# Sending all of the attention branch's gated output tiles through the seven-product form in a streaming-encoder trunk

## Chip, cores and metric

The kernel runs on one core of a Trainium2 chip. The metric is the device time of one launch in microseconds (us); lower is better.

## What is computed

Two layers over 640 tokens (512 of a new stream and 8 x 16 of running streams) with 1024 features. The part of the reference that matters here is the end of the mixer:

```python
g = jax.nn.sigmoid(g + b_gate)
g_conv, g_attn = jnp.split(g, 2, axis=-1)
y_conv, conv_new = _short_conv(cb, cc, cv, conv_prev, w_conv)
...
m = g_conv * (y_conv @ w_conv_out) + g_attn * (y_attn @ w_attn_out)
return m @ w_o, conv_new, k_new, v_new
```

`y_conv` and `y_attn` have 512 columns; `g_conv`, `g_attn`, `m` and the result have 1024. Ahead of the mixer and behind it stands a SwiGLU block. All is float32.

## The kernel before

**Layout and products.** Features lie on the 128 partitions and tokens on the free axis, so a tile is 128 x 640, split where needed into two token halves of 320. Every operand is split into a rounded part `hi` and a remainder `lo` (ACT casts `hi`, DVE subtracts to get `lo`), and a product is three matmuls (hi·hi, hi·lo, lo·hi). Weights are split on the chip in the same way, slab by slab.

**Seven products.** Most large products are done by Winograd's variant of Strassen's scheme: two output rows by two token halves need seven block products instead of eight. For that the right-hand operand needs, beside its four blocks, four mixtures: `XT5`, `XN6`, `XT7` and `XT4`. The weights need mixtures too: two slabs arrive by DMA, DVE adds halves of them, and a third part is made in DRAM-to-SBUF transfers that accumulate (tile `one`, on POOL's queue).

**The units.** In `outputs` three kinds of units follow each other. A *gate unit* (`gate_pair(m)`, tiles `qa`, `qb`, `qc`) makes two gate tiles by seven block products of 12 matmuls. A *rows unit* (`rows`, tiles `ra`, `rb`, `rc`) makes four output tiles by seven products of 12 matmuls. A plain tile (`out(m)`, tile `py`) takes 24 matmuls. Before, the order from the eighth gate on is: four times a gate unit and two plain tiles of the attention branch. The conv branch has four plain tiles and one rows unit for the other four; that unit stands just ahead of gate unit 8. Behind them `po` (the product with `w_o`) takes the eight mixed tiles `m_0` to `m_7`, 48 matmuls for each output.

**What sets the order.** `outputs` is written in a hand-set order for PE, DVE and ACT: each engine runs its instructions in the order in which the code names them. Within a unit, `prep` casts the next weight slab on ACT, `flush` takes its remainder on DVE, `ahead` adds the halves of a coming slab on DVE, and `at[0..2]` are places in a gate unit (after its first, fourth and fifth product) where the caller hangs other work. `due` runs what an earlier unit put off. SP's queue loads the slabs (`raw`, three buffers and a wait for the oldest to be read), POOL's the `one` tiles (two buffers).

Of the kernel before, what the change touches and what calls it, by code (L numbers as in the profile page):

```python
# [11 lines left out]
F32R = mybir.dt.float32r  # L12
# [4 lines left out]
P = 128  # L17
# [111 lines left out]

# [57 lines left out]
def two(ps):  # L187
    return ps[:, :, :HT]


def halves(t):
    return t.rearrange("p (a b) -> p a b", a=2)
# [3 lines left out]
def trunk(ctx: ExitStack, tc: tile.TileContext, xin, wst, small, pbias, samplebias, kcache, vcache, gfin,  # L196
# [24 lines left out]
    def acc(name):  # L221
        return banks["acc"].tile([P, 2, 512], F32, tag="acc", name=name)
# [1110 lines left out]
    def mixer(l, after):  # L1333
        with tc.tile_pool(name=f"yp{l}", bufs=1, reuse_waits="tile") as yp, \
# [84 lines left out]
            with tc.tile_pool(name=f"gp{l}", bufs=1, reuse_waits="tile") as gp, \  # L1419
                 tc.manual_schedule(engines=ORDERED):  # L1420
# [3 lines left out]
        with tc.manual_schedule(engines=ORDERED):  # L1424
            hold[0] = True
            for m in range(KT):
                po = acc(f"po{l}_{m}")
                product(po, mo)
                ex.weights(m)
                DVE.tensor_tensor(out=halves(x[m]), in0=two(po), in1=halves(x[m]), op=ALU.add)  # L1430
                if m < KT - 1:
                    flush()
                ex.final(m)
        return ex

    class Operands:
# [48 lines left out]
    def outputs(l, gp, X, st, cs, ycp, yas, sigmoid, gates):  # L1485
# [20 lines left out]
        def gate_pair(m, at):  # L1506
            n = f"{l}_{m}"
            pa, pb, pc = (att(f"q{i}{n}")[:, :HT] for i in "abc")
            u, g = gates[m], gates[m + 1] = tmp(f"g{n}"), tmp(f"g{n}_1")
            s0 = quiet()  # L1510
            block(pa, s0, 0, X11, every, True, True)
            ACT.copy(c1, pa)
            due()
            prep(used[0] + 1)
# [9 lines left out]
            ACT.copy(c5, pc)  # L1524
# [4 lines left out]
            DVE.tensor_tensor(out=g[:, t2], in0=g[:, t2], in1=rr[:, t2], op=ALU.mult)  # L1529
# [35 lines left out]
            if post:  # L1565
                post()

        yc, ya, mo = [], [], []
        more = []
        yas_ = [yas[:, c, :] for c in range(CT)]  # L1570
# [5 lines left out]
        def give(ms):  # L1576
            for m in ms:
                mo.append(parts(hp, "h", f"m{l}_{m}", mm[m]))
# [4 lines left out]
        def mixed(i, y, z):  # L1583

            z = z.rearrange("p c (a b) -> p (c a) b", a=2)
            e1, e2, o1, o2 = (z[:, i] for i in range(4))
            add(e1, e1, e2, ALU.subtract)
            add(e2, o2, e2, ALU.subtract)
            for out, a in ((o2, e1), (o1, o2)):
                DVE.scalar_tensor_tensor(out=out, in0=a, scalar=-1.0, in1=out, op0=ALU.mult, op1=ALU.subtract)  # L1590
            yield
            hi, lo = (gp.tile([P, 3, HT], F32R, tag=f"x{i}{p}", name=f"x{p}{l}_{len(more)}") for p in ("hi", "lo"))
            ACT.copy(hi, z[:, 1:])
            more.append((hi, lo))
            yield
            low(lo, z[:, 1:], hi)
            yield
            hi, lo = (u[:, t2] for u in y[2 * i])
            ACT.copy(hi, e1)
            yield  # L1600
            low(lo, e1, hi)
            yield

        def take_even(c, src):
            y = tuple(gp.tile([P, T], F32R, tag=f"y{c}{i}", name=f"ya{l}_{c}{i}") for i in ("hi", "lo"))
            split(*(z[:, t1] for z in y), src[:, t1])
            ya.append(y)

        EXTRA = XT7, XT4, XN6

        def kind(y, i, k):
            if k in EXTRA:
                return tuple(z[:, EXTRA.index(k)] for z in more[i - 2])
            hi, lo = y[2 * i + (k in (X21, X22))]
            return tuple(z[:, t2 if k in (X22, XT5) else t1] for z in (hi, lo))

        def rows(name, ms, y, then=None):

            n = f"{name}{l}_{ms[0]}"
            gs = [gates[m + (KT if name == "ao" else 0)] for m in ms]  # L1620
# [5 lines left out]
            def mul(ps, s, half, k, start):  # L1626
                for u in range(2):
                    for i in range(2):
                        kp = half * NP + 2 * u + i
                        wh, wl = (z[:, kp * P : (kp + 1) * P] for z in s)  # L1630
                        xh, xl = kind(y, i, k)
# [20 lines left out]
            due()  # L1652
            prep(used[0] + 1)
            flush()
            mul(b, w, 1, X21, True)
            add(s1, two(B), s1)
            w = slab(True)[0]
# [1 line left out]
            mul(a, w, 0, XN6, False)  # L1659
            ACT.copy(s2, two(A))  # L1660
            gated(0, [s1[:, u] for u in range(2)], t1)
            mul(c, w, 1, XT5, True)
            for u in range(2):
                ACT.copy(s5[:, u], c[u])
# [2 lines left out]
            add(s5, two(A), s5)  # L1667
            flush()
            ahead()
            gated(1, [s5[:, u] for u in range(2)], t2, -1.0)  # L1670
# [10 lines left out]
            flush()  # L1681
            gated(1, a, t1, -1.0)
            if name == "co":
                lates.append(lambda: moved(1))

        def total(m0, m1):
            for m in range(m0, m1):
                add(mm[m], mm[m], gates[KT + m])

        none = lambda: None  # L1690

        def also(*fs):
            return lambda: [f() for f in fs]

        def going(z):
            return lambda: next(z)

        gate_pair(2, [none, none, lambda: take(yc, "yc", range(CT), ycs)])
        z = [mixed(i, yc, ycp[i]) for i in range(2)]
        out(0, yc, None, going(z[0]))  # L1700
        out(1, yc, None, also(going(z[0]), going(z[1])))
        out(2, yc, None, also(going(z[0]), going(z[1])))
        out(3, yc, None, going(z[1]))
        both = also(going(z[0]), going(z[1]))
        gate_pair(4, [both, both, none])
# [665 lines left out]
```

## Time and profile before

| | |
|---|---|
| median of 3 runs | 2486.89 us (2486.20 to 2486.92) |
| the profiled execution | 2487.08 us, span 2485.3 us |
| PE (TensorE matmul) | 2471.0 us busy, 99% of the span |
| DVE (VectorE) | 2158.3 us, 87% |
| ACT (ScalarE) | 1373.0 us, 55% |
| POOL (GpSimd) | 317.4 us, 13% |
| DMA | 287.11 MB, 116 GB/s in the mean |

The profiled execution lasts 1.8 us longer than its span. A row of the timeline gives start, duration, engine, line, operation, output and inputs. On DVE and ACT the duration of an instruction is longer than the distance to the next one's start, since ends overlap; where a queue is summed up, that distance is what counts. A block is twelve matmuls of 128 x 320.

### The profile page before, as it was taken

To read this page: it belongs to the slowest core of one execution; us is meant where nothing else is said; L and a number is where in the kernel's file an instruction comes from. 1 tells how busy PE (TensorE), PEld (TensorE's weight loads), DVE (VectorE), ACT (ScalarE), POOL (GpSimd) and SP (SyncE) were. 2 spreads that over 40 slices of the span, in tenths; PEclk is the share of its full clock that TensorE was granted. 3 is DMA by queue.
4 is the path that set the end of the run, shared out by engine and by line. 5 is a ranking of instruction groups with operands and counts; after the bars stand their busy time and mean duration, and the time that the engine had idled before them with its cause. 6 is when DMAs were issued, how large, how long until landed. Compare 5 with 4: busy or idle time off the path is not lost.

```text
span 2485.3 us, 43991 instructions
## 1 busy us (share of the span) xinstructions
PE 2471.0 (99%) x17288; PEld 2418.2 (97%) x17288; DVE 2158.3 (87%) x3587; ACT 1373.0 (55%) x2196; POOL 317.4 (13%) x479
## 2 busy tenths in 40 slices
PE   9999999999999999999999999999999999999999
PEld 8999999889999999999999999998999999999998
DVE  7999998888886899998799999988878769999997
ACT  6555556665554555555665555556645455555555
POOL 0111112211000001111001111121110000111111
PEclk9999999999999999999999999999999999999999
DMA  4443445335343334444334443453453333443444
GB/s 155 126 118 102 123 119 121 113 109 177 104 118 108 94 101 106 112 117 120 108 94 109 110 118 102 116 128 107 132 173 92 115 111 89 107 116 106 113 117 117
DMA packets 113072, 287.11 MB, mean 116 GB/s; under 512 B 12928, under 2 KB 52480, under 8 KB 112864
## 3 DMA queue, kind: packets, MB, share of 16 engines
q1 hardware_dynamic: 69552, 220.10, 28.0%
q0 software_dynamic: 42880, 63.94, 13.7%
q8 instruction: 135, 2.21, 0.4%
q14 instruction: 73, 0.60, 0.1%
q10 hardware_dynamic: 432, 0.25, 0.0%
HBM read 238.43 MB, written 7.94 MB: 99 GB/s over the span
## 4 chain that ended last, share of the span: by engine, by line
PE 92%; DVE 4%; ACT 2%; DMA 1%; issue 1%; SPq 0%; DVEq 0%; ACTq 0%; POOLq 0%
PE pab L458 12%; PE paa L458 11%; PE pcb L458 6%; PE daa L1143 6%; PE pca L458 5%; PE dab L1143 5%; PE po L434 5%; PE qa L458 4%; PE py L434 3%; PE pbb L458 3%; PE dca L1143 3%; PE pba L458 3%; PE dcb L1143 2%; PE ma_qk L458 2%; PE ma_cv L458 2%; PE pv L1770 2%
## 5 line engine op out<-in xcount | busy, mean ns | idle before, releaser
L363 ACT CAST whi<-raw 128x512 fp32r<-128x512 f32 (+1 forms) x573 | 500.4, 878 | 371.3 <-PE pbb L458 46.0
L368 DVE TENSOR_TENSOR wlo<-raw,whi 128x512 fp32r<-128x512 f32 (+1 forms) x573 | 574.4, 1005 | 135.9 <-ACT whi L363 132.1
L363 ACT CAST whi<-s 128x1024 fp32r<-128x1024 f32 (+1 forms) x160 | 151.6, 947 | 313.3 <-issue 111.4
L458 PE MATMUL pab<-xhib,whi 128*128 128x320 f32 x704 | 217.5, 309 | 0.0
L458 PE MATMUL pab<-xlob,whi 128*128 128x320 f32 x704 | 217.0, 308 | 0.0
L458 PE MATMUL pab<-xhib,wlo 128*128 128x320 f32 x704 | 217.0, 308 | 0.0
L458 PE MATMUL paa<-xhia,whi 128*128 128x320 f32 x640 | 197.7, 309 | 0.2 <-DVE ga L295 0.2
L458 PE MATMUL paa<-xhia,wlo 128*128 128x320 f32 x640 | 197.5, 309 | 0.0
L458 PE MATMUL paa<-xloa,whi 128*128 128x320 f32 x640 | 197.4, 308 | 0.0
L368 DVE TENSOR_TENSOR wlo<-s,whi 128x1024 fp32r<-128x1024 f32 (+1 forms) x160 | 174.8, 1092 | 4.6 <-ACT whi L363 4.6
L1165 POOL DMA_DIRECT2D x<-c_a x80 | 70.0, 1022 | 573.8 <-ACT ahia L1047 205.5
L1165 POOL DMA_DIRECT2D x<-c_b x72 | 62.8, 1002 | 583.6 <-ACT ahib L1047 205.8
L458 PEld LDWEIGHTS pab<-xhib,whi 128*128 128x128 f32 x704 | 132.1, 188 | 0.9 <-issue 0.9
L458 PEld LDWEIGHTS pab<-xlob,whi 128*128 128x128 f32 x704 | 132.2, 188 | 0.0
L458 PEld LDWEIGHTS pab<-xhib,wlo 128*128 128x128 f32 x704 | 132.1, 188 | 0.0
L458 PEld LDWEIGHTS paa<-xhia,whi 128*128 128x128 f32 x640 | 120.1, 188 | 1.1 <-DVE ga L295 0.5
L458 PEld LDWEIGHTS paa<-xloa,whi 128*128 128x128 f32 x640 | 120.1, 188 | 0.2 <-DVE xloa L702 0.2
L458 PEld LDWEIGHTS paa<-xhia,wlo 128*128 128x128 f32 x640 | 120.1, 188 | 0.2
L295 DVE TENSOR_TENSOR raw<-s,raw 128x512 f32<-128x512 f32 x160 | 109.1, 682 | 0.0
L458 PE MATMUL pcb<-xhib,wlo 128*128 128x320 f32 x352 | 108.7, 309 | 0.0
L458 PE MATMUL pcb<-xlob,whi 128*128 128x320 f32 x352 | 108.5, 308 | 0.0
L458 PE MATMUL pcb<-xhib,whi 128*128 128x320 f32 x352 | 108.5, 308 | 0.0
(840 smaller groups left out, 8150.4 us busy)
## 6 DMA issues: line engine op xcount, KB each, us to landing
raw<-in_wst SPq DMA_DIRECT2D x375, 512.0 KB, 3.6
x<-c_a POOLq DMA_DIRECT2D x80, 160.0 KB, 4.6
x<-c_b POOLq DMA_DIRECT2D x72, 160.0 KB, 3.6
lent<-in_wst POOLq DMA_DIRECT2D x36, 256.0 KB, 3.9
kc<-in_kcache SPq DMA_DIRECT2D x32, 256.0 KB, 5.2
vc<-in_vcache SPq DMA_DIRECT2D x16, 512.0 KB, 4.8
one<-in_wst POOLq DMA_DIRECT2D x28, 256.0 KB, 4.1
x<-u_a POOLq DMA_DIRECT2D x40, 160.0 KB, 4.1
```

The lines of the kernel that those rows point to most:

```text
L295: DVE.tensor_tensor(out=out, in0=a, in1=b, op=op)
L363: ACT.copy(hi[:, d], src[:, c])
L368: DVE.tensor_tensor(out=lo, in0=src, in1=hi.bitcast(F32), op=ALU.subtract)
L434: PE.matmul(ps[:, a, :HT], w, x[a] if isinstance(x, tuple) else x[:, a * HT : (a + 1) * HT], start=first and j == 0 and not seeded, stop=l ...
L458: PE.matmul(ps, a, b, start=start and kp == 0 and j == 0, stop=stop and kp == NP - 1 and j == 2, skip_group_check=True)
L1143: PE.matmul(ps[u], w, y, start=start and i == 0 and j == 0, stop=i == 1 and j == 2, skip_group_check=True)
L1165: POOL.dma_start(x[ms[2 * u + r]][:, cols], z[:, u], accum_op=ALU.add)
L1770: PE.matmul(pv[t], xx[:, t * P : (t + 1) * P], w[:, kk * AW : (kk + 1) * AW], start=c == 0 and kk == 0 and j == 0, stop=c == KT // 2 - 1 a ...
```

## The change

All eight output tiles of the attention branch are made by two rows units (tiles 0 to 3 and 4 to 7). The order from gate unit 8 on becomes: gate units 8 and 10, rows unit 0 to 3, gate units 12 and 14, rows unit 4 to 7.

```diff
-    for i in range(4):
-        out += [gates[4 + i], ("ao", 2 * i), ("ao", 2 * i + 1)]
+    for i in range(2):
+        out += gates[4 + 2 * i : 6 + 2 * i] + [("rows", ("ao", tuple(range(4 * i, 4 * i + 4))))]
```

The mixtures of the attention output `ya` are made in place by four DVE instructions 128 x 2 x 320 wide (`mix`), cast on ACT (`high`) and subtracted on DVE (`rest`) into tiles of their own (`xhi`, `xlo`; `room`). The calls are hung on the units:

```diff
-        rows("co", (4, 5, 6, 7), yc)
-        for m in range(KT, 2 * KT, 2):
-            last = m == 2 * KT - 2
-            gate_pair(m, [none, none, (lambda: take(ya, "ya", range(CT), yas_)) if m == KT else
-                          (lambda: give(range(1))) if last else none])
-            out(m, ya, (lambda: give(range(1, 4))) if last else None)
-            out(m + 1, ya, (lambda: give(range(4, 6))) if last else None)
-        give(range(6, KT))
+        rows("co", (4, 5, 6, 7), None)
+        gate_pair(8, [none, lambda: (moves[0](), take_even(0), take(ya, "ya", [1], srcs)),
+                      lambda: (take_even(2), take(ya, "ya", [3], srcs))])
+        room("ao")
+        gate_pair(10, [lambda: (mix(0), mix(1)), lambda: (mix(2), high(XT5), high(XN6)),
+                       lambda: (mix(3), rest(XN6), high(XT7))])
+        rows("ao", (0, 1, 2, 3), lambda: (rest(XT5), high(XT4)), lambda: rest(XT7), lambda: rest(XT4), False, True)
+        gate_pair(12, [lambda: total(0, 1), moves[1], lambda: total(2)])
+        pre = lambda: total(3)
+        gate_pair(14, [pre, lambda: (begun(*range(4)), given(0, 2)), none])
+        rows("ao", (4, 5, 6, 7), None, lambda: given(1, 3), None, True)
+        begun(*range(4, KT))
+        total(4, 5)
+        given(4)
+        total(6, 7)
+        given(5, 6, 7)
```

`rows` gains the hooks `first`, `mid` and `late`, the switch `defer` (two gatings of the first attention unit are put off to gate unit 12), and its conv unit no longer copies two finished tiles (`moved(0)`) ahead of its last product; they go to the `due` of gate unit 8, the other two to `moves[0]`:

```diff
-            if then:
-                then()
-            if name == "co":
-                moved(0)
             mul(a, w, 0, XT4, False)
-            flush()
+            if not end:
+                flush()
             gated(1, a, t1, -1.0)
             if name == "co":
-                lates.append(lambda: moved(1))
+                lates.append(lambda: moved(0))
+                moves.append(lambda: moved(1))
```

In `mixer` the two ordered blocks become one, and the first two `po` tiles are begun together: both take `m_0`, `m_2`, `m_1`, `m_3`, then both take the rest.

```diff
+        first = [acc(f"po{l}_{m}") for m in range(2)]
+        ws = [[tiles.take() for _ in mo] for _ in first]
+        for ks in ((0, 2, 1, 3), range(KT // 2, KT)):
+            for p, w in zip(first, ws):
+                for k in ks:
+                    multiply(p, w[k], mo[k], k == 0, k == KT - 1)
```

On ACT, at the middle of gate unit 8 (the copies out of `qa` and `qc`, `c` and `capsm` being the copies' targets), there stood before:

```order
L1522 COPY capsm_4817<-qa_8_7988 128x320
L1524 COPY c_4829<-qc_8_7990 128x320
L363 CAST whi_8060<-raw_8058 128x1024
L234 CAST ya_0hi<-ya_4760 128x640
L234 CAST ya_1hi<-ya_4760 128x640
L234 CAST ya_2hi<-ya_4760 128x640
L234 CAST ya_3hi<-ya_4760 128x640
```

In the changed kernel ACT has at the same place of gate unit 8 (`yc_1` and the two `g_6` are the finished tiles of the conv branch that are moved):

```order
L1530 COPY capsm_4817<-qa_8_7996 128x320
L1532 COPY c_4829<-qc_8_7998 128x320
L1688 COPY yc_1_4820<-g_6_7746 128x640
L1688 COPY yc_1_4820<-g_6_1_7747 128x640
L234 CAST ya_0hi<-ya_4760 128x320
L234 CAST ya_1hi<-ya_4760 128x640
L363 CAST whi_8078<-raw_8076 128x1024
L234 CAST ya_2hi<-ya_4760 128x320
L234 CAST ya_3hi<-ya_4760 128x640
```

Two copies and two of the `ya` casts now stand ahead of the cast of the next unit's first slab, and DVE's remainders of `ya_0` and `ya_1` stand ahead of its add out of `qa`.

On DVE, from gate unit 10's add out of `qb` on, there stood before (`rrm` is the normalisation's factor, `s` a sum of weight halves):

```order
L295 TENSOR_TENSOR g_10_8200<-qb_10_8198,capsm_4817 128x320
L368 TENSOR_TENSOR wlo_8236<-raw_8130,whi_8235 128x512
L295 TENSOR_TENSOR g_10_1_8201<-qa_10_8197,c_4829 128x320
L1529 TENSOR_TENSOR g_10_1_8201<-g_10_1_8201,rrm_4818 128x320
L368 TENSOR_TENSOR wlo_8268<-raw_8265,whi_8267 128x1024
L295 TENSOR_TENSOR g_10_8200<-qc_10_8199,capsm_4817 128x320
L1536 TENSOR_TENSOR g_10_8200<-g_10_8200,rrm_4818 128x640
L1542 TENSOR_TENSOR g_10_1_8201<-qa_10_8197,rrm_4818 128x320
```

In the changed kernel DVE has there, up to the add out of `qc` (`ya` written and read alone is a `mix`, `xloao_2` the remainder of `XN6`):

```order
L295 TENSOR_TENSOR ya_4760<-ya_4760 128x2x320 x2
L295 TENSOR_TENSOR g_10_8169<-qb_10_8152,capsm_4817 128x320
L368 TENSOR_TENSOR wlo_8194<-raw_8096,whi_8193 128x512
L1599 SCALAR_TENSOR_TENSOR ya_4760<-ya_4760 128x2x320
L295 TENSOR_TENSOR g_10_1_8170<-qa_10_8151,c_4829 128x320
L1537 TENSOR_TENSOR g_10_1_8170<-g_10_1_8170,rrm_4818 128x320
L368 TENSOR_TENSOR wlo_8230<-raw_8227,whi_8229 128x1024
L295 TENSOR_TENSOR raw_8247<-raw_8247 128x512
L295 TENSOR_TENSOR s_106_8252<-raw_8247,raw_8227 128x512
L1599 SCALAR_TENSOR_TENSOR ya_4760<-ya_4760 128x2x320
L1591 TENSOR_TENSOR xloao_2_8150<-ya_4760,xhiao_2_8149 128x640
L295 TENSOR_TENSOR g_10_8169<-qc_10_8153,capsm_4817 128x320
```

Four mixtures, one wide remainder and the sums of the next rows unit's weights now stand between instructions on which the unit's own products wait.

On ACT, in gate unit 10 behind its copy out of `qc`, the changed kernel has:

```order
L1532 COPY c_4829<-qc_10_8153 128x320
L1643 CAST ya_0hi<-ya_4760 128x320
L1643 CAST ya_2hi<-ya_4760 128x320
L1643 CAST xhiao_2_8149<-ya_4760 128x640
L363 CAST whi_8229<-raw_8227 128x1024
L1643 CAST xhiao_0_8145<-ya_4760 128x640
```

The cast `whi` of the rows unit's first slab stands behind the cast of `XN6`, which reads what DVE's third `mix` writes; before, that `whi` followed the copy out of `qc`.

More of the change, by code (lines that the diff above doesn't have):

```diff
@@ L1423, in mixer @@
         ex = after()
[L1424 to L1427, printed above, removed]
-                product(po, mo)
-                ex.weights(m)
-                DVE.tensor_tensor(out=halves(x[m]), in0=two(po), in1=halves(x[m]), op=ALU.add)
-                if m < KT - 1:
-                    flush()
-                ex.final(m)
+        hold[0] = True
+        first = [acc(f"po{l}_{m}") for m in range(2)]
[4 more added lines that the diff above has]
+                    multiply(p, w[k], mo[k], k == 0, k == KT - 1)
+        for m in range(KT):
+            po = first[m] if m < 2 else acc(f"po{l}_{m}")
+            if m > 1:
+                product(po, mo)
+            ex.weights(m)
+            DVE.tensor_tensor(out=halves(x[m]), in0=two(po), in1=halves(x[m]), op=ALU.add)
+            if m < KT - 1:
+                flush()
+            ex.final(m)
+        order.close()
         return ex
@@ L1566, in out @@
                 post()
-        yc, ya, mo = [], [], []
-        more = []
-        yas_ = [yas[:, c, :] for c in range(CT)]
+        yc, ya = [], []
+        mo = [None] * KT
+        srcs = [yas[:, c, :] for c in range(CT)]
+        x, moves = {}, []
         def take(y, name, cs, srcs):
@@ L1602, in mixed, with mix, place, high @@
             yield
[L1604 to L1607, printed above, removed]
+        za = yas.rearrange("p (i c) (a b) -> p i (c a) b", i=2, a=2)
+        def mix(n):
+            e1, e2, o1, o2 = (za[:, :, k] for k in range(4))
+            if n == 0:
+                add(e1, e1, e2, ALU.subtract)
+            elif n == 1:
+                add(e2, o2, e2, ALU.subtract)
+            else:
+                minus(*((o2, e1) if n == 2 else (o1, o2)))
+        def place(k):
+            if k == XT5:
+                return [(*(u[:, t2] for u in ya[2 * i]), za[:, i, 0]) for i in range(2)]
+            return [(*x["ao", k], za[:, :, 1 + EXTRA.index(k)])]
+        def high(*ks):
+            for k in ks:
+                for hi, _, z in place(k):
+                    ACT.copy(hi, z)
+        def rest(*ks):
+            for k in ks:
+                for hi, lo, z in place(k):
+                    low(lo, z, hi)
         EXTRA = XT7, XT4, XN6
-        def kind(y, i, k):
+        def kind(name, i, k):
             if k in EXTRA:
-                return tuple(z[:, EXTRA.index(k)] for z in more[i - 2])
-            hi, lo = y[2 * i + (k in (X21, X22))]
+                return tuple(z[:, i] for z in x[name, k])
+            hi, lo = (yc if name == "co" else ya)[2 * i + (k in (X21, X22))]
             return tuple(z[:, t2 if k in (X22, XT5) else t1] for z in (hi, lo))
-        def rows(name, ms, y, then=None):
+        def rows(name, ms, first, mid=None, late=None, end=False, defer=False):
             n = f"{name}{l}_{ms[0]}"
@@ L1669, in rows @@
             ahead()
-            gated(1, [s5[:, u] for u in range(2)], t2, -1.0)
+            if defer:
+                moves.append(lambda: gated(1, [s5[:, u] for u in range(2)], t2, -1.0))
+            else:
+                gated(1, [s5[:, u] for u in range(2)], t2, -1.0)
+            if late:
+                late()
             mul(c, w, 1, X22, False)
@@ L1690, in outputs, with total, begun, given @@
+            if end:
+                flush()
+        def total(*ms):
+            for m in ms:
+                add(mm[m], mm[m], gates[KT + m])
+        def begun(*ms):
+            for m in ms:
+                mo[m] = tuple(hp.tile([P, T], F32R, tag=f"h{i}", name=f"m{l}_{m}{i}") for i in ("hi", "lo"))
+        def given(*ms):
+            for m in ms:
+                split(*mo[m], mm[m])
         none = lambda: None
[L1692 to L1696, printed above, removed]
+        def going(*zs):
+            return lambda: [next(z) for z in zs]
```

61 lines of the change are left out of this document (36 added, 25 removed).

## The prediction

> **What bounds the kernel now.** I read the page first. Its line 1 shows PE without air and DVE second:
>
> ```profile
> span 2485.3 us, 43991 instructions
> PE 2471.0 (99%) x17288; PEld 2418.2 (97%) x17288; DVE 2158.3 (87%) x3587; ACT 1373.0 (55%) x2196; POOL 317.4 (13%) x479
> ```
>
> Then the busy time by stretches, around the place of the change (layer 0): the conv branch's rows unit, the stretch from gate unit 8 to the first `po`, and inside it gate unit 12 alone. Columns are the stretch, its length, busy PE, PEld, DVE, ACT and POOL, granted clock, DMA share and GB/s.
>
> ```profile
> 686.40:698.72 12.32, 12.32 (x86) 12.32 (x85) 10.31 (x18) 7.23 (x12) 1.43 (x2) 1.00 0.49 129
> 698.72:776.75 78.03, 77.85 (x530) 77.30 (x529) 59.74 (x93) 40.41 (x64) 3.43 (x5) 1.00 0.36 105
> 738.01:750.31 12.30, 12.30 (x86) 12.30 (x86) 7.88 (x12) 4.93 (x8) 0.00 (x0) 1.00 0.29 89
> ```
>
> PE is busy in all of it. DVE has 10.31 of 12.32 us in a rows unit and 7.88 of 12.30 us in a gate unit; in the whole stretch 59.74 of 78.03 us. A rows unit is the fullest thing that DVE does here, and the change puts two more of them into a shorter stretch.
>
> The chain that ended last gives PE's pace (start, us, what):
>
> ```profile
> 702.52 2.03 PE qa L458 x12
> 706.30 1.81 PE qa L458 x12
> ...
> 718.66 1.76 PE qa L458 x12
> ...
> 730.97 7.04 PE py L434 x48
> ```
>
> A block of twelve matmuls takes 1.76 us, so one matmul 0.1467 us; a unit of seven blocks takes 12.31 us (718.66 to 730.97), two plain tiles 7.04 us. Two blocks are longer, 2.03 and 1.81 us. The timeline of PE shows what is left of waiting:
>
> ```profile
> 702.09 0.31 PE L458 MATMUL qb<-hhim,wlo 128*128 128x320 f32 x1
> 702.52 0.41 PE L458 MATMUL qa<-thi,whi 128*128 128x320 f32 x1
> 702.77 0.31 PE L458 MATMUL qa<-tlo,whi 128*128 128x320 f32 x1
> ...
> 776.23 0.46 PE L434 MATMUL py<-ya_3hi,wlo 128*128 128x320 f32 x2
> 776.75 0.53 PE L434 MATMUL po<-m_0hi,whi 128*128 128x320 f32 x2
> ...
> 782.10 0.46 PE L434 MATMUL po<-m_6hi,whi 128*128 128x320 f32 x2
> 782.46 0.56 PE L434 MATMUL po<-m_6lo,whi 128*128 128x320 f32 x2
> ```
>
> In gate unit 8 a hole of 0.28 us (0.43 less 0.15) before 702.52, and the matmul behind it takes 0.25 instead of 0.15 until the next starts: 0.38 us, and 0.05 us at 706.30. At the start of `po` about 0.33 us (776.52 to 776.75 and the slower restart), at `m_6` 0.17 us. All else in the stretch is PE's own pace.
>
> **What goes.** Eight plain tiles were 192 matmuls, two rows units are 168: 24 x 0.1467 = 3.52 us less PE work in a layer. That is the whole direct gain. The hole in gate unit 8 goes too. It came from ACT:
>
> ```profile
> 700.79 1.35 ACT L1647 COPY yc<-g 128x640 f32<-128x640 f32 x2 [0.78 <-DVE g L1640]
> 702.05 0.41 ACT L1512 COPY capsm<-qa 128x320 f32<-128x320 f32 x1
> ...
> 706.34 0.43 ACT L1524 COPY c<-qc 128x320 f32<-128x320 f32 x1 [0.31 <-PE qc L458]
> 706.66 1.05 ACT L363 CAST whi<-raw 128x1024 fp32r<-128x1024 f32 x1
> 707.61 0.72 ACT L234 CAST ya_0hi<-ya 128x640 fp32r<-128x640 f32 x1
> 708.24 0.73 ACT L234 CAST ya_1hi<-ya 128x640 fp32r<-128x640 f32 x1
> ```
>
> The copy out of `qa` (702.05) stood behind two copies of finished tiles (700.79); with `moved(0)` put off it comes first. I take 0.43 us off for this, and 0.17 us for `m_6`, as `m_4` to `m_7` are now needed only 7.04 us after `po` begins. The 0.33 us at the start of `po` may stay: between 0 and 0.33.
>
> **What DVE has to do.** Distances between starts, from DVE's timeline:
>
> ```profile
> 721.00 0.82 DVE L295 TENSOR_TENSOR mm<-mm,g 128x640 f32<-128x640 f32 x1
> 721.74 0.69 DVE L295 TENSOR_TENSOR raw<-s,raw 128x512 f32<-128x512 f32 x1
> 722.34 0.68 DVE L368 TENSOR_TENSOR wlo<-one,whi 128x512 fp32r<-128x512 f32 x1
> 723.11 0.69 DVE L368 TENSOR_TENSOR wlo<-raw,whi 128x512 fp32r<-128x512 f32 x1
> 723.72 0.48 DVE L295 TENSOR_TENSOR g<-qb,capsm 128x320 f32<-128x320 f32 x1
> 724.12 0.68 DVE L368 TENSOR_TENSOR wlo<-raw,whi 128x512 fp32r<-128x512 f32 x1
> ...
> 727.56 0.49 DVE L295 TENSOR_TENSOR g<-qa,c 128x320 f32<-128x320 f32 x1 [2.76 <-PE qa L458]
> 728.09 0.49 DVE L1529 TENSOR_TENSOR g<-g,rrm 128x320 f32<-128x320 f32 x1
> 728.50 1.22 DVE L368 TENSOR_TENSOR wlo<-raw,whi 128x1024 fp32r<-128x1024 f32 x1
> 729.63 0.48 DVE L295 TENSOR_TENSOR g<-qc,capsm 128x320 f32<-128x320 f32 x1
> ```
>
> So an instruction 640 wide takes 0.74 us of the queue, 512 wide 0.60, 320 wide 0.40, 1024 wide 1.13; 0.12 more when it reads what the one before it wrote (727.56 to 728.09), and 0.16 more once in a unit where the second half of a lent slab is cast late (722.34 to 723.11). By these a gate unit is 9.0 us (0.40 x 5, 0.60 x 8, 0.74, 1.13, 0.36) and a rows unit 11.8 us, against PE's 12.3. On top come, unit by unit: gate unit 8 the remainders of `ya`, 2 x 0.40 + 2 x 0.74 = 2.3; gate unit 10 four `mix` and a wide remainder, 5 x 0.74 + 0.12 = 3.8; rows unit 0 to 3 the other remainders, 2 x 0.40 + 2 x 0.74 = 2.3, less two gatings put off, 0.8. That is 11.3, 12.8 and 13.3 us for 12.3 us each. DVE falls behind, and the products of the rows unit wait for it by name: `xlo` of `XN6`, `XT5`, `XT7`, `XT4`.
>
> The forms 128 x 2 x 320 do not occur before; I price them as 640-wide rows, 0.74 (nearest). Bounds: 0.60 (the 512 row) and 0.80 (two 320 rows).
>
> **The path, step by step**, in the clock of before. Gate unit 8 starts at 702.09 + 0.15 - 3.52 = 698.72; without waits its blocks end every 1.76 us, rows unit 0 to 3 at 698.72 + 3 x 12.32 = 735.7.
>
> First, ACT. Its width-320 cast is
>
> ```profile
> L1599 ACT CAST yc_0hi<-yc 128x320 fp32r<-128x320 f32 x1 | 0.5, 454 | 0.0
> ```
>
> thus about 0.36 between starts. The fourth block ends at 705.76. ACT copies `qc` (0.32), moves two tiles (1.31), casts `ya_0` (0.36) and `ya_1` (0.73 to its end): 708.5. DVE waits for these, subtracts (0.74), and reaches its add out of `qa` at 709.3; the seventh block waits for it until 709.85, where 709.28 was due. The instruction queued behind on ACT is the cast of the next slab, and on DVE everything.
>
> Second, DVE from 709.33 to `mix(2)`, 20 instructions: six of 320 (2.40), eight of 512 (4.80), five of 640 (3.70), one of 1024 (1.13), four dependent (0.48), 0.16: 12.67, so to 722.0, and 0.12 to its end. PE meanwhile waits about 0.8 us in gate unit 10 for the remainder of the summed weights.
>
> Third, ACT: the cast of `XN6` (0.63) and only then the rows unit's first slab (1.05): 723.9. DVE, which has two short instructions to do, stands 0.9 us.
>
> Fourth, DVE from 723.9 to the remainder of `XT7`, 20 instructions: 1024 once (1.13), eight of 512 (4.80), four of 640 and one to its end (2.96 + 0.82), six of 320 (2.40), 0.40 as above: 12.5, to 736.4. On the way PE waits for `XN6`, for the slab's remainder and for `XT5`; its block with `XT7` goes on at 736.45 and ends at 738.17 (1.71 us).
>
> Fifth, DVE has to add out of that block before it goes on (0.74), then a slab's remainder (1.13), two weight sums (0.60 + 0.72), and the remainder of `XT4` (0.82): 742.2. PE's last block ends at 743.97.
>
> So rows unit 0 to 3 ends at 743.97 where 735.68 is PE's own pace: 8.3 us of new waiting in a layer. Gate units 12 and 14 and rows unit 4 to 7 carry 12.0, 11.2 and 11.9 us of DVE work by the same prices, less than 12.3, so I see none there, and `m_5` is ready 0.2 us ahead of its use in `po`, the tightest place; if that cover goes, up to 0.5 us.
>
> **Transfers.** Two rows units load as many slabs as four plain ones; two pairs of accumulating `one` transfers a layer are added on POOL's queue.
>
> ```profile
> raw<-in_wst SPq DMA_DIRECT2D x27, 512.0 KB, 4.4
> one<-in_wst POOLq DMA_DIRECT2D x10, 256.0 KB, 4.2
> ```
>
> A pair needs 2 x 4.2 us, a buffer is free a unit (12.3 us) ahead, and the rows unit of before runs at 129 GB/s with the same pattern. I cost them at nothing; without that cover a late pair is some 4 us.
>
> **The sum.** Per layer -3.52 - 0.43 - 0.17 + 8.29 = +4.17, or +3.84 if the start of `po` loses its hole; I take 4.1. The second layer runs the same code and is taken as the same, so twice: +8.2 us. Against the profiled execution (2487.08, of which 2485.3 is the span) that is 2495.3; against the median 2486.89, 0.19 lower, 2495.1. Seven wide forms lie on DVE's path; at 0.60 they take 1.0 us off a layer, at 0.80 they add 0.4, and the tail may add 0.5: 2.8 (without the hole at `po`) to 5.1. Some 45 instructions, each read to about 0.02 us, may be 0.9 us off in all: 1.9 to 6.0 a layer, 2490.7 to 2498.9.
>
> **Rivals.**
> Faster: DVE keeps pace and the mixtures are ready a unit ahead; then only what goes counts, -4.1 to -4.4 a layer, 2478.3. It needs DVE's list from 709.3 to the remainder of `XT4` (32.9 us with its waits) to fit in PE's 24.6 us to that block. For it speaks only that DVE is at 77% over the stretch; against it, that the surplus sits in three units in a row. 0.05.
>
> The same: ACT's casts are always ready, so that steps one and three and the wait in step five cost DVE nothing. DVE then adds out of `qa` at 707.6, when the fifth block is done, and its 45 instructions sum to 30.0 us: 737.6 instead of 742.2, 4.6 less, -0.5 a layer, 2485.9. For it: ACT is busy 40.41 of 78.03 us. Against: at each of these places the cast stands behind an instruction that itself waits. 0.10.
>
> Much slower: the holes lower PE's clock. At the start of the program, after idle time, matmuls are slow at first:
>
> ```profile
> 5.60 0.63 PE L434 MATMUL poa<-xhia,whi 128*128 128x320 f32 x1 [5.60 <-ACT whi L758]
> ...
> 6.30 0.47 PE L434 MATMUL poa<-xloa,whi 128*128 128x320 f32 x1
> 6.57 0.47 PE L434 MATMUL poa<-x2loa,whi 128*128 128x320 f32 x1
> ...
> 11.61 0.31 PE L434 MATMUL poa<-xhia,whi 128*128 128x320 f32 x1
> 11.76 0.31 PE L434 MATMUL poa<-x2hia,whi 128*128 128x320 f32 x1
> ```
>
> They come 0.27 us apart instead of 0.15; the 24 matmuls from 5.60 to 11.61 took 6.01 us for 3.52, 2.5 us lost. Once in each layer that gives +5.0 more, 2500.1. Against: the hole of 0.28 us at 702.52 left the next matmuls at 0.15, and the longest hole that I work out is 2.2 us (before the last block) with blocks of matmuls between. 0.04. [...]
>
> That the change does not do what it says is no rival: the 24 matmuls are gone from PE's order.
>
> **How the numbers follow.** The forecast has 0.81, the rivals 0.05, 0.10 and 0.04. The smallest difference that a measurement of this kernel tells is about 0.2%, 5.0 us: faster is below 2481.9, slower above 2491.9. Of the forecast's range its lowest edge (0.04) falls within 0.2%: faster 0.05, same 0.14, slower 0.81. The range 2490.5 to 2499.0 is the forecast's own; the three rivals outside it hold 0.19.
>
> **What would show it.** PE's work down by 48 matmuls of 0.1467 us; no long block at the third product of gate unit 8; one at its seventh, released by DVE's add out of `qa`; in rows unit 0 to 3 waits of 0.7 to 2.2 us at the blocks of `XN6`, `XT5`, `XT7` and `XT4`, all released by DVE; none in gate units 12 and 14. It is wrong if PE waits less than 5 us in these three units, if the waits are released by ACT or DMA, if `po` waits for `m_4` to `m_7` by more than 1 us, or if matmuls behind a hole come 0.27 us apart.

## The result, and the profile after

The changed kernel took 2497.07 us in the median of five runs (2495.55 to 2498.37), the kernel before 2486.36 us (2486.13 to 2486.92) beside it. The ratio is 1.0042, 95% interval 1.0031 to 1.0053: slower by 0.42%, and the interval lies above the 0.2% bound. The profiled execution took 2495.55 us, 8.47 us more than that of before (2487.08).

The head of the page (span; engine, busy time, share, instructions):

```profile
span 2493.7 us, 44059 instructions
PE 2467.2 (99%) x17240; PEld 2411.1 (97%) x17240; DVE 2193.6 (88%) x3673; ACT 1392.1 (56%) x2246; POOL 322.5 (13%) x487
```

PE has 48 matmuls fewer (17288 to 17240), and the span is still 8.4 us longer: PE now waits. Where, the stretches around the change say (columns as in the prediction):

```profile
698.94:781.49 82.55, 75.88 (x506) 73.91 (x505) 73.72 (x125) 47.77 (x82) 5.73 (x8) 1.00 0.36 105
706.00:746.00 40.00, 33.33 (x216) 31.40 (x216) 34.71 (x58) 22.23 (x38) 3.72 (x5) 1.00 0.41 119
744.68:757.00 12.32, 12.32 (x87) 12.32 (x86) 10.21 (x19) 3.88 (x7) 1.43 (x2) 1.00 0.44 129
```

From gate unit 8 to `po` PE stands still for 6.67 us, and all of it lies in the 40 us from gate unit 8's fifth block to just behind rows unit 0 to 3 (PE is busy for 33.33 of 40.00). The stretch from 744.68, gate unit 12, has none. The starts of the layer's first `qa` and of its first `po`,

```profile
635.63 0.31 PE L458 MATMUL qa<-hhim,whi 128*128 128x320 f32 x1
...
781.49 0.46 PE L434 MATMUL po<-m_0hi,whi 128*128 128x320 f32 x2
```

are 145.86 us apart; before it was 776.75 - 635.42 = 141.33, so layer 0 grew by 4.5 us. In layer 1 the same distance went from 141.47 to 145.86, 4.4 more. The rest of the program is the same to 0.6 us.

What PE waits for in the whole program (who, for which product of which line: us in total, times, longest):

```profile
PE raao L1674 <- DVE xloao L1591: 7.0, 4, 2.3
...
PE rcao L1674 <- DVE ya_0lo L1591: 2.2, 2, 1.1
PE qa L458 <- DVE wlo L368: 1.1, 2, 0.6
PE raao L1674 <- ACT capsm L1692: 1.0, 2, 0.5
PE qa L458 <- DVE g L295: 1.0, 2, 0.5
PE raao L1674 <- DVE wlo L368: 1.0, 2, 0.5
```

The row left out here is a wait at the program's start, there before too; rows of 0.5 us in all and less, which follow, are left out as well. Each of the others stands for one wait in each layer, the first for two. Of their 13.3 us, 9.2 are waits for the remainders (`xloao`, `ya_0lo`) of three mixtures, `XT5`, `XT7` and `XT4`. The chain of waits through rows unit 0 to 3 (start, us, what) runs over DVE almost without a break:

```profile
707.84 0.36 ACT ya_0hi L234
708.20 0.64 ACT ya_1hi L234
...
708.87 0.82 DVE ya_1lo L235
709.70 0.41 DVE g L295
...
723.07 1.05 ACT whi L363
...
724.14 1.23 DVE wlo L368
...
735.95 0.75 DVE xloao L1591
...
736.74 1.89 PE raao L1674 x11
...
738.73 0.06 DVE rs L295
...
742.01 0.75 DVE xloao L1591
...
742.80 1.88 PE raao L1674 x11
```

These are the places of the prediction's five steps: ACT's casts of `ya`, DVE to `mix(2)`, ACT's slab cast, DVE to the remainder of `XT7`, and the round over PE's block to the remainder of `XT4`.

### The profile page after: what moved, and what is told of

The parts are those of the page before. It is cut to its first block, busy times and chain, and to the rows that moved or that the text cites. A ratio compares the mean times of both kernels' runs of the same rounds, so it can differ in the third digit from the quotient of the medians.

```text
span 2493.7 us, 44059 instructions
## 1 busy us (share of the span) xinstructions
PE 2467.2 (99%) x17240; PEld 2411.1 (97%) x17240; DVE 2193.6 (88%) x3673; ACT 1392.1 (56%) x2246; POOL 322.5 (13%) x487
## 4 chain that ended last, share of the span: by engine, by line
PE 91%; DVE 5%; ACT 2%; issue 1%; DMA 1%; SPq 0%; DVEq 0%; ACTq 0%; POOLq 0%
PE pab L458 12%; PE paa L458 11%; PE pcb L458 6%; PE daa L1143 6%; PE pca L458 5%; PE dab L1143 5%; PE po L434 5%; PE qa L458 3%; PE pbb L458 3%; PE dca L1143 3%; PE pba L458 3%; PE dcb L1143 2%; PE ma_cv L458 2%; PE ma_qk L458 2%; PE pv L1833 2%; PE qc L458 2%
```

## The experiments

The theory: PE waits because DVE's instructions for the mixtures stand, in a fixed order, ahead of what the running unit needs, and twice DVE stands itself behind a cast of ACT. Rivals: that another part of the change costs the time (copies put off, the common start of two `po`, the single block); that the mixtures' own arithmetic is too much for DVE; that holes lower PE's clock. Each run's ratio is to the kernel before, run beside it on the same chip (2486.4 to 2486.6 us). The changed kernel itself ran again only beside e6 to e8 (it is e5), so where e1 to e4 are set against its 2497.07 us, that is across runs.

**e1: the attention branch's tiles plain again**, the other parts of the change kept:

```diff
-    for i in range(2):
-        out += gates[4 + 2 * i : 6 + 2 * i] + [("rows", ("ao", tuple(range(4 * i, 4 * i + 4))))]
+    for i in range(4):
+        out += [gates[4 + i], ("ao", 2 * i), ("ao", 2 * i + 1)]
...
+        gate_pair(8, [none, moves[0], lambda: take(ya, "ya", range(CT), srcs)])
+        out(8, ya)
+        out(9, ya)
...
```

> The eight attention tiles are plain again; the put-off copies, the common start of the first two po tiles and the single ordered block are kept. Queue theory (DVE and ACT fall behind in gate units 8, 10 and rows unit 0 to 3, the rest of the change is a small gain): the hole in gate unit 8 (0.43 us) and the one at m_6 (0.17 us) go in each layer, up to 0.33 us more at the start of po, so 1.2 to 1.9 us below the kernel before, some 2485 us. Rival 'tail' (the loss is in the common start of po and the single block): it stays slower than before by several us, and PE waits for m_4 to m_7 or at the start of po.

2485.79 us (2485.50 to 2486.66), ratio 0.9997 [0.9988, 1.0005]; 0.85 us below the kernel before, where 1.2 to 1.9 were expected. The other parts cost nothing: the whole loss comes with the rows units. The stretch from first `qa` to first `po` is 0.65 and 0.74 us shorter than before, about what the holes in gate unit 8 and at the start of `po` had taken; of that 1.4 us, 0.66 was lost again in the stretch from layer 0's first `po` to layer 1's first `pv` (881.93 before, 882.59 here), most of which has the same code. That stretch took 881.8 to 882.6 in all profiles, so I do not read a cause into it.

**e2: ACT's order**, two edits: the two copies of finished tiles behind the casts of `ya_0` and `ya_1`, and `XN6`'s cast one place later, behind the slab's:

```diff
-        gate_pair(8, [none, lambda: (moves[0](), take_even(0), take(ya, "ya", [1], srcs)),
-                      lambda: (take_even(2), take(ya, "ya", [3], srcs))])
+        gate_pair(8, [none, lambda: (take_even(0), take(ya, "ya", [1], srcs)),
+                      lambda: (moves[0](), take_even(2), take(ya, "ya", [3], srcs))])
...
-                       lambda: (mix(2), high(XT5), high(XN6)),
-                       lambda: (mix(3), rest(XN6), high(XT7))])
+                       lambda: (mix(2), high(XT5)),
+                       lambda: (high(XN6), mix(3), rest(XN6), high(XT7))])
```

> Only the place of two groups of ACT instructions is changed in the changed kernel: in gate unit 8 the two copies of finished tiles go behind the casts of ya_0 and ya_1 and the next slab, in gate unit 10 the cast of XN6 goes behind the cast of the rows unit's first slab. The same instructions run. Queue theory: the 0.5 us hole at the seventh block of gate unit 8 goes, DVE's 0.9 us wait for that slab's cast goes, the wait for XN6 goes; worked through the rows of the queues 2.1 us less waiting in each layer, 4 us in all below the changed kernel, about 2492 us. Rival 'amount' (DVE has more to do than PE in these units, in whatever order): no change against the changed kernel, 2495 to 2497 us. Rival 'transfers' (the two added pairs of accumulating transfers): no change.

2493.02 us (2492.59 to 2494.94), ratio 1.0026 [1.0016, 1.0037]; 4.0 us of the loss are gone. The timeline of DVE in e2 shows both steps. The add out of `qa` comes at 708.12 (709.61 in the changed kernel), and the slab's remainder at 721.76 begins without waiting (in the changed kernel at 724.14, after 0.82 us of waiting for `whi`):

```profile
706.75 0.49 DVE L235 TENSOR_TENSOR ya_0lo<-ya,ya_0hi 128x320 fp32r<-128x320 f32 x1 [0.62 <-ACT ya_0hi L234]
707.38 0.82 DVE L235 TENSOR_TENSOR ya_1lo<-ya,ya_1hi 128x640 fp32r<-128x640 f32 x1
708.12 0.48 DVE L295 TENSOR_TENSOR g<-qa,c 128x320 f32<-128x320 f32 x1
...
721.76 1.22 DVE L368 TENSOR_TENSOR wlo<-raw,whi 128x1024 fp32r<-128x1024 f32 x1
```

Steps one and three are shown to cost about 2 us a layer: layer 1 took 143.81 us from `qa` to `po` for 145.86. Layer 0 took 145.25. There something else happened in the profiled execution. The timeline of PE from the hole on:

```profile
740.44 0.41 PE L1674 MATMUL raao<-xloao,whi 128*128 128x320 f32 x1 [2.27 <-DVE xloao L1591]
...
741.72 0.36 PE L1674 MATMUL raao<-xhiao,whi 128*128 128x320 f32 x1
741.88 0.47 PE L1674 MATMUL raao<-xloao,whi 128*128 128x320 f32 x1
...
745.08 0.40 PE L458 MATMUL qa<-hlom,whi 128*128 128x320 f32 x1
745.31 0.30 PE L458 MATMUL qa<-hhim,wlo 128*128 128x320 f32 x1
```

Behind the hole before the last block, from 741.88 to 745.08, twelve matmuls come 0.267 us apart instead of 0.147: 1.4 us lost. It is the sign that the prediction named for its rival of the clock. Layer 1 of the same run has a hole of the same length before its last block and no such row behind it.

**e3: the remainder of `XT4` one hook sooner**, ahead of DVE's wait for the block of `XT7`:

```diff
-        rows("ao", (0, 1, 2, 3), lambda: (rest(XT5), high(XT4)), lambda: rest(XT7), lambda: rest(XT4), False, True)
+        rows("ao", (0, 1, 2, 3), lambda: (rest(XT5), high(XT4)), lambda: (rest(XT7), rest(XT4)), None, False, True)
```

> Only one DVE instruction is moved in the changed kernel: in rows unit 0 to 3 the remainder of XT4 is taken behind that of XT7, ahead of the add out of the fifth block, a 1024-wide slab remainder and two weight sums, instead of behind them. Queue theory: the longest hole (2.2 to 2.4 us, before the last block) goes, the others stay: 2.2 to 2.5 us a layer, 4.5 to 5 us below the changed kernel, about 2491.5 us. Rival 'amount': DVE must do the same work before the next gate unit, so the hole comes back later in gate unit 12; no change beyond 1 us.

2490.28 us (2489.96 to 2491.43), ratio 1.0016 [1.0007, 1.0025]: 6.8 us less than the changed kernel, more than the 4.5 to 5 expected. In the profile the layers are 2.5 us shorter each, the whole of the longest hole. What PE waits for:

```profile
PE raao L1674 <- DVE xloao L1591: 2.5, 2, 1.3
```

where 7.0 us stood, four times. The profiled executions differ by 5.3 us, so the surplus of the medians lies in executions that left no trace. I put it down to the clock (below): with the longest hole gone, few stretches can be idle enough. That is argued, not shown.

**e4: the four `mix` left out** (casts and remainders stay):

```diff
-        gate_pair(10, [lambda: (mix(0), mix(1)), lambda: (mix(2), high(XT5), high(XN6)),
-                       lambda: (mix(3), rest(XN6), high(XT7))])
+        gate_pair(10, [none, lambda: (high(XT5), high(XN6)), lambda: (rest(XN6), high(XT7))])
```

> The four instructions that make the mixtures of ya are left out (casts and remainders are taken of the unmixed tiles), so the attention branch is not computed as it should be. That is 3.1 us less DVE work in each layer and ACT's cast of XN6 no longer waits for DVE. Queue theory: 1.9 us less waiting in each layer (the holes at XN6 go, those at XT5, XT7 and XT4 stay since their remainders still stand behind the adds out of the blocks), 4 us below the changed kernel. Rival 'amount': the whole 3.1 us comes off each layer, 6 us in all. Rival 'transfers': no change.

2494.46 us (2492.81 to 2496.67), ratio 1.0032 [1.0019, 1.0045]; 2.6 us less than the changed kernel, where 4 were expected, and a wide spread. The profiled execution (2495.69) has in layer 0 a stretch at half clock, as e2 had one: 3.41 us at 0.50 from 741.21 on, behind 3.41 us in which PE was busy for 1.14. Its mean clock of 0.998, for 0.999 in e2, fits one more in layer 1. Less some 1.5 us for each of these (estimated from the 0.267 us a matmul of e2: 3.41 us hold 12.8 of them, 1.88 us of work at 0.147), the layers (145.54 and 145.97 us) are 1.8 and 1.4 us shorter than the changed kernel's, near the 1.9 expected. So the mixtures' arithmetic explains a part only; without it most of the loss stays, since casts and remainders keep their places.

**e5: the changed kernel again**, no edit.

> The changed kernel once more, unchanged, for a second profile and for its spread beside the other runs of this chip. Its runs lay 2495.55 to 2498.37 us apart, three times as wide as those of the kernel before. Queue theory: the same holes at the same blocks, 8 to 9 us a layer, with lengths that differ by a few tenths; what the slower runs have more lies in these units. Rival 'elsewhere': the holes are the same to 0.1 us and the difference lies in the blocks around, where nothing was changed.

2497.35 us (2495.36 to 2498.34), ratio 1.0042 [1.0030, 1.0055], as in the first five runs. The profiled execution took 2496.51 us, 0.96 more than that of the first five. Its holes are the same to 0.02 us and its layers last 145.93 and 145.86 us; the first `qa` starts at 636.54 instead of 635.63. So here the rival 'elsewhere' is right: 0.9 us of the difference lies ahead of everything that the change touches. Of the slower executions (2497 to 2498 us) there is no trace.

**e6: the remainder of `XN6` taken three times:**

```diff
-                       lambda: (mix(3), rest(XN6), high(XT7))])
+                       lambda: (mix(3), rest(XN6), rest(XN6), rest(XN6), high(XT7))])
```

> The changed kernel with the remainder of XN6 taken three times instead of once in gate unit 10 (same values): two more 640-wide DVE instructions on the path, 1.48 us a layer. Queue theory: DVE's list is the path here, so each comes through in full and the wait at XN6 grows; with its knock-on about 1.5 to 1.7 us a layer, 3.0 to 3.4 us above the changed kernel run beside it. Rival 'ACT': DVE waits for ACT's casts anyway, the addition is partly hidden, under 1.5 us in all.

2501.52 us (2500.83 to 2502.51), ratio 1.0061 [1.0048, 1.0073]; 4.2 us over e5, where 3.0 to 3.4 were expected. The two extra instructions do arrive at PE: in e6 the block of `XN6` waits for ACT's copy out of `raao`, which stands behind DVE's queue,

```profile
PE raao L1674 <- ACT capsm L1692: 4.5, 2, 2.2
```

for 1.0 before, 1.75 us a layer. The surplus I put down to the clock again; stretches of e6 (columns as above, the seventh is the granted clock):

```profile
727.75:731.16 3.41, 1.18 (x8) 0.92 (x7) 3.31 (x6) 0.88 (x2) 0.00 (x0) 1.00 0.00 0
731.16:734.57 3.41, 3.08 (x12) 2.67 (x12) 3.34 (x7) 3.27 (x6) 0.51 (x1) 0.50 0.00 0
```

A stretch of 3.41 us with eight matmuls in it (23 fit) is followed by one of 3.41 us at a granted clock of 0.50. Layer 0 has a second such pair: eight matmuls in the 3.41 us from 741.41 (PE busy for 1.14), then 0.50 from 744.82 to 748.23. The first lies ahead of the wait for `XT5`, 1.1 us in the changed kernel and gone from the rows of e6, and so costs little. The mean clock of the execution is 0.997, for 1.000 in the changed kernel, and each layer is 3.2 to 3.3 us longer than the changed kernel's (149.13 and 149.10), 1.5 us beyond the longer wait.

**e7: all eight by seven, with most of the waits taken out**: ACT's order of e2, and the remainders of `XT5`, `XT7` and `XT4` each a place sooner:

```diff
...
+            if early:
+                early()
             prep(used[0] + 1)
...
-        rows("ao", (0, 1, 2, 3), lambda: (rest(XT5), high(XT4)), lambda: rest(XT7), lambda: rest(XT4), False, True)
+        rows("ao", (0, 1, 2, 3), lambda: (rest(XT7), high(XT4)), lambda: rest(XT4), None, False, True,
+             lambda: rest(XT5))
```

> All eight attention tiles by seven as in the change, with ACT's order of the second experiment and the remainders in the order in which PE needs them: XT5's ahead of the lent slab's, XT7's ahead of the add out of the second block, XT4's in the place of XT7's. The same instructions as the changed kernel. Queue theory: the holes at XT7 and XT4 go, 2.4 us of waiting is left in a layer (weight remainders in gate unit 10 and at XN6, and one at XT7's cast), so 2.1 us a layer below the kernel before, about 2482 us. Rival 'amount': 37.4 us of DVE work for 36.9 us of PE in three units leaves no gain: not below 2486 us.

2483.20 us (2482.19 to 2483.96), ratio 0.9986 [0.9977, 0.9995], 14 us below the changed kernel with the same instructions and the same transfers. So the loss is one of order, not of amount. Some waiting is left, 1.8 us in both layers together for ACT's copy ahead of the block of `XT7` and 0.9 us for a slab's remainder, and the time is 1.2 us above the 2482 expected.

**e8: only the last four tiles by seven.** Tiles 0 to 3 stay plain, and the mixtures are spread over two gate units and four plain tiles:

```diff
     for i in range(2):
-        out += gates[4 + 2 * i : 6 + 2 * i] + [("rows", ("ao", tuple(range(4 * i, 4 * i + 4))))]
+        out += [gates[4 + i], ("ao", 2 * i), ("ao", 2 * i + 1)]
+    out += gates[6:] + [("rows", ("ao", (4, 5, 6, 7)))]
...
+        out(8, ya, None, lambda: mix(0))
+        out(9, ya, None, lambda: mix(1))
+        gate_pair(10, [lambda: mix(2), lambda: (mix(3), high(XN6)), none])
+        out(10, ya, None, lambda: (rest(XN6), high(XT7)))
+        out(11, ya, None, lambda: (rest(XT7), high(XT4)))
+        gate_pair(12, [lambda: high(XT5), lambda: rest(XT4), lambda: rest(XT5)])
...
```

> Only the last four attention tiles by seven; the first four plain, two behind gate unit 8 and two behind gate unit 10, where DVE has time between its adds; mixtures, casts and remainders are spread over these plain tiles and gate unit 12, all ready a unit ahead of rows unit 4 to 7. 12 matmuls (1.76 us) less in a layer instead of 24. Queue theory: no new hole, 1.76 + 0.43 + 0.17 = 2.4 us a layer, 4.7 to 5.3 us below the kernel before, about 2481.6 us, the fastest of all. Rival 'amount' expects no holes either; rival 'transfers' expects half of the loss of the change, 2491 us.

2481.58 us (2481.15 to 2483.61), ratio 0.9981 [0.9973, 0.9990]: the fastest of all, 4.9 us below before. It saves half as many matmuls, and PE has no wait in the stretch (busy PE is the second number):

```profile
698.50:774.50 76.00, 76.00 (x521) 75.94 (x520) 68.48 (x110) 44.54 (x74) 4.29 (x6) 1.00 0.37 108
```

**e9 and e10: the clock by itself.** Both are e8 with extra remainders of mixtures that change no value, e9 eight of `XT4` in gate unit 12, e10 three of `XN6` in gate unit 10 and six of `XT4` in gate unit 12. The edit of e9 against e8:

```diff
-        gate_pair(12, [lambda: high(XT5), lambda: rest(XT4), lambda: rest(XT5)])
+        gate_pair(12, [lambda: high(XT5), lambda: (rest(XT4), *(rest(XT4) for _ in range(8))), lambda: rest(XT5)])
```

> The half version (only tiles 4 to 7 of the attention branch by seven), with the remainder of one mixture taken nine times instead of once in gate unit 12; the values stay the same. Worked out by the prices of the queue: eight extra instructions of 0.74 us and their dependence use up the spare time of DVE and leave one hole of 3.15 us in PE in each layer at the seventh block of gate unit 12 (and 0.37 us in gate unit 14), +1.2 us a layer against the kernel before. Theory 'queue only': before + 2.4, about 2488.9 us, the same as the version with two holes. Theory 'clock': a window of 3.41 us in which PE is busy for less than some 0.4 is followed by one at half clock, 1.5 us each; the hole of 3.15 us covers 0.6 of a window in about three of four alignments, so 0 to 2 such windows a run, 1.5 on the mean: 2490 to 2492 us, runs spread over up to 3 us, and matmuls 0.27 us apart behind the hole in a profile.

> The half version with nine extra remainders of mixtures as well, three in gate unit 10 and six in gate unit 12; the values stay the same. By the prices of the queue two holes of 1.39 and 1.66 us in each layer, each at a seventh block, and again +1.2 us a layer. Theory 'queue only': before + 2.4, about 2488.9 us, the same as the version with one hole. Theory 'clock': no hole covers 0.6 of a window (2.05 us), so no window at half clock: 2488.9 us too, narrow, and 1 to 3 us less than the version with one hole; no matmuls 0.27 us apart.

e9: 2492.95 us (2491.93 to 2493.78), ratio 1.0026 [1.0016, 1.0036]. e10: 2489.97 us (2489.52 to 2491.33), ratio 1.0014 [1.0005, 1.0023]. By what DVE's queue makes PE wait they are alike: 6.6 us in e9, and in e10 6.0 us and another 0.4 for a slab's remainder. The waits for DVE's add out of `qa` in e9 and then in e10:

```profile
PE qa L459 <- DVE g L296: 6.6, 2, 3.3
```

```profile
PE qa L459 <- DVE g L296: 6.0, 4, 1.6
```

And yet e9 takes 3.0 us more, and the mean clock of its profiled execution is 0.997, for 0.999 in that of e10. In its timeline of PE twenty matmuls behind the hole of layer 0, from 752.03 to 757.37, stand 0.267 us apart, and of the stretches around it (second fence) two of 3.41 us in a row are granted 0.50:

```profile
751.60 0.64 PE L459 MATMUL qa<-thi,whi 128*128 128x320 f32 x1 [3.29 <-DVE g L296]
752.03 0.47 PE L459 MATMUL qa<-tlo,whi 128*128 128x320 f32 x1
...
757.10 0.43 PE L459 MATMUL qa<-hhim,wlo 128*128 128x320 f32 x1
757.37 0.32 PE L459 MATMUL qa<-hhim,whi 128*128 128x320 f32 x1
```

```profile
747.12:750.53 3.41, 1.19 (x9) 0.93 (x7) 3.27 (x5) 0.00 (x0) 0.00 (x0) 1.00 0.62 107
750.53:757.36 6.83, 5.76 (x21) 5.76 (x22) 6.72 (x12) 1.15 (x2) 0.00 (x0) 0.50 0.00 0
```

In e10 the matmuls behind the hole of 1.57 us keep their pace, and the clock stays at 1.00 behind a stretch of 3.41 us that held thirteen:

```profile
752.41 0.41 PE L459 MATMUL qa<-thi,whi 128*128 128x320 f32 x1 [1.57 <-DVE g L296]
752.66 0.31 PE L459 MATMUL qa<-tlo,whi 128*128 128x320 f32 x1
```

```profile
748.97:752.38 3.41, 1.87 (x13) 1.60 (x11) 3.28 (x5) 0.00 (x0) 0.21 (x1) 1.00 0.70 174
752.38:757.00 4.62, 4.59 (x31) 4.59 (x32) 4.54 (x8) 1.47 (x3) 0.00 (x0) 1.00 0.00 0
```

The theory "queue only" falls: the same waiting in one piece costs 3.0 us more than in two, and the clock of 0.50 is seen behind the hole in the one and not behind the hole of 1.57 us in the other. Both times are about 1 us above what was expected (2490 to 2492 us for e9, 2488.9 for e10); each layer of e10 is 0.4 us longer than worked out, which I leave open.

## Why the prediction was right

The sign, the place and the mechanism were as forecast, and 2495.1 us is within 0.5 of the profiled execution, 2.0 below the median. By its steps, where all times of the prediction are to be read 0.21 us later, since the changed kernel's layer began that much later (635.63 for 635.42):

- **PE's work and the holes that go**: 48 matmuls fewer, as said. No long block is left in gate unit 8 before its seventh; `po` goes through its first 24 matmuls pair by pair without a hole (0.29 us a pair from 781.49 on), so the 0.33 us at its start went as well. The chosen 4.1 a layer had left this open; with it the sum is 3.84.
- **Steps one to four** came to within 0.15 us: DVE's add out of `qa` at 709.61 (709.5), the slab's remainder at 724.14 (724.1), PE's block with `XT7` on at 736.74 (736.66). e2 shows steps one and three to be worth 2 us a layer.
- **Step five was about 0.3 us short.** The prediction let DVE add when the block of `XT7` ended at PE's pace, 738.38 by the clock of after. The rows of DVE say otherwise:

```profile
738.73 0.82 DVE L295 TENSOR_TENSOR rs<-raao,rs 128x640 f32<-128x640 f32 x1 [2.04 <-PE raao L1674]
739.47 1.21 DVE L368 TENSOR_TENSOR wlo<-raw,whi 128x1024 fp32r<-128x1024 f32 x1
```

PE had started on the next block 0.27 us before:

```profile
738.46 0.31 PE L1674 MATMUL rcao<-ya_1hi,whi 128*128 128x320 f32 x1
```

Here the next block started 0.27 us before the result of the one before was read, and the term lacked that. The trace of before has the same 0.27 us: DVE's add at 727.56, which the prediction shows, waited for a block whose successor PE began at 727.29.

```profile
727.29 0.31 PE L458 MATMUL qc<-hhim,whi 128*128 128x320 f32 x1
```

Rows unit 0 to 3 therefore ended at 744.52, where 744.18 was worked out: 8.63 us of new waiting for the 8.29 of the sum, 0.08 of the difference brought along from step four. That the forecast still came so near the profiled execution is in part luck: the chosen 4.1 is 0.26 more than the 3.84 that holds with the hole at `po` gone, and this nearly made up for the term.
- **The wide forms**, priced 0.74: two `mix` from 718.98 to 720.58, thus 0.80 each with the dependence, and 0.74 between starts for the others. The price was right.

```profile
718.98 1.68 DVE L295 TENSOR_TENSOR ya<-ya 128x640 f32<-128x640 f32 x2
720.58 0.48 DVE L295 TENSOR_TENSOR g<-qb,capsm 128x320 f32<-128x320 f32 x1
```

- **The releasers**: one of the waits in rows unit 0 to 3 was for ACT, not DVE (0.5 us, the copy out of `raao`), which the prediction had named as a sign of being wrong. That copy waited in its turn for DVE's add out of `qc`, so the path is DVE's queue all the same. The place, the block of `XN6`, was right, the name was not: the remainder of `XN6` itself was done at 728.17, ahead of that block's start at 729.42. The holes were 0.7 to 2.4 us long instead of 0.7 to 2.2.
- **Gate units 12 and 14, transfers**: no waits there, and none for a transfer in any of them.
- **The rival of the clock was priced too low in its chance.** The prediction gave it 0.04, on the ground that the longest hole was 2.2 us. In e2, e4 and e6 the clock was at 0.50 for 3.41 us behind stretches of that length in which PE was busy for 1.39 (e2), 1.14 (e4), 1.18 and 1.14 us (e6). In the two profiled executions of the changed kernel it was at 1.00 behind the longest hole, and these took 2495.55 and 2496.51 us; its ten runs lie between 2495.36 and 2498.37. The four at a mean clock of 1.000 are the four fastest (to 2496.51), the six at 0.999 the slowest (2497.07 on). One stretch of 3.41 us at half clock lowers that mean by 0.0007 (half of 3.41 in 2497 us) and, by the estimate at e4, costs some 1.5 us, so I take the median's 2 us above the sum to be one or two such stretches in most runs. For the changed kernel itself this is argued: no trace of it holds one, the kernel before shows both readings of the clock too (in its profiled execution the 0.999 comes from the last 3.1 us of the span alone, at 0.50), and of the two profiled executions the slower lost its 0.9 us ahead of the first `qa`. That e2, e4, e6 and e9 lose time in this way is shown.

## What to carry to other kernels

Before saving matmuls with instructions on a second engine, sum that engine's queue unit by unit, in its order, not over the stretch: DVE was at 77% over the stretch and still last in three units running. The same instructions cost 11 us in one order and won 3 us in another (e7), and half of the change with no wait at all won most (e8). When an instruction waits for a block of matmuls, add the time from the start of the next block until the result can be read (0.27 us here). Split a hole that can't be avoided; here one of 3.3 us in each layer cost 3 us more over two layers than two of half the length.

## What the runs showed of the hardware

In layer 0 of e2 PE's clock was at 0.50 for 3.41 us behind a hole of 2.43 us. The stretches at 0.50 that were read around the changed units lasted 3.41 us (e2 from 741.83, e4 from 741.21, e6 from 731.16 and from 744.82) or 6.83 us (e9 from 750.53); the two of e6 begin 13.66 us apart, four times 3.41. Stretches of 3.41 us with 11 matmuls (1.66 us busy, e5, below) and with 13 (1.87 us, e10) had full clock behind them. Ahead of those at 0.50 stood 3.41 us at full clock with eight matmuls (1.14 us busy in e4 and in e6, 1.18 in e6) or nine (1.19 us in e9, 1.39 in e2):

```profile
738.42:741.83 3.41, 1.39 (x9) 1.39 (x10) 3.38 (x7) 1.14 (x2) 0.00 (x0) 1.00 0.00 0
741.83:745.24 3.41, 3.41 (x15) 3.41 (x14) 2.76 (x6) 0.00 (x0) 0.00 (x0) 0.50 0.00 0
```

(e2: the hole of 2.43 us from 737.86 to 740.44 fell for 2.0 us into the first stretch.) In e5, the changed kernel, 3.41 us around the same hole held 11 matmuls and the clock stayed at 1.00:

```profile
742.03:745.44 3.41, 1.66 (x11) 1.66 (x12) 3.38 (x8) 1.14 (x2) 0.00 (x0) 1.00 0.00 0
745.44:748.85 3.41, 3.41 (x25) 3.41 (x24) 2.90 (x6) 1.39 (x3) 0.00 (x0) 1.00 0.00 0
```

So behind a hole of 2.4 us the clock was at 0.50 in layer 0 of e2, where 1.4 us were lost, and at 1.00 in e5. That this depends on where the hole lies against the borders between the stretches is argued, not shown: around e5's hole no change of the clock marks a border. What e2 shows is that a stretch of 3.41 us in which PE was still busy for 1.39 us was followed by one at 0.50, so a hole as long as the whole stretch was not needed there.
